# Sums of squares moved from GpSimd to VectorE at the sublayer boundaries, and the filter's last layer in the split format

## The chip, the cores and the metric

The kernel runs on one core of a Trainium2 chip. The metric is the time of one execution on the device in microseconds (us), as the median of three runs. Engines are named as the profile names them: PE is TensorE (the matrix engine; PEld its weight loads), DVE is VectorE, ACT is ScalarE, POOL is GpSimd, and SP is SyncE, whose queue issues most of the DMA transfers.

## The reference

Two layers of an encoder on 512 tokens of width 1024, in float32. Each layer has a mixer and a gated feed-forward block with a convolution, and each of these four sublayers is wrapped in a norm before and a norm after it:

```python
def rms_norm(x, gain):
    y = xf * lax.rsqrt(jnp.mean(xf * xf, axis=-1, keepdims=True) + EPS)
    return y * gain
...
for layer in range(DEPTH):
    h = rms_norm(x, mix_pre_norm[layer])
    m = even_mixer(h, ...) if layer % 2 == 0 else odd_mixer(h, ...)
    x = x + rms_norm(m, mix_post_norm[layer])
    h = rms_norm(x, ffn_pre_norm[layer])
    f = conv_ffn(h, ...)
    x = x + rms_norm(f, ffn_post_norm[layer])
```

The even mixer is latent attention beside neighbourhood attention on an 8 by 64 grid; the odd one is retention beside a Hyena operator, a long convolution done with Fourier transforms. The Hyena filters do not depend on x. They come out of a small network over the 512 positions with a window on its output:

```python
h = jnp.sin(freq * (z @ w1 + b1))
...
h = h @ w4                      # 512 x 64 times 64 x 1024
return h[:, :HY_WIDTH] * window, h[:, HY_WIDTH:] * window
```

## The kernel before, in words

**Tiles.** x and every h are eight tiles of 128 features by 512 tokens. A matrix product in the split format runs three matmuls for each 128x128 block of weights, in `mm` (L280 to L282): high part by high part, high part of the weights by low part of h, low part of the weights by high part of h. Weights arrive by DMA on SP's queue into `raw` (128x1024), and ACT makes the high part `whi` (L259) and DVE the low part `wlo` (L260). There are four buffers of weights, and three are loaded ahead.

**A boundary between two sublayers** (`boundary`, called four times; the last has no following sublayer and the change leaves it as it is). The columns are worked in two halves of 256 tokens, `ca` and `cb`. The products of the last sublayer end with half ca, its norm's statistic is taken (`stats`: matmuls with a column of ones L292, a mean on DVE L295 or L297, a power on POOL L299), the factor is spread over all partitions by PE transposes (`spread`, L316), and `update(ca)` runs for each of the eight tiles: DVE multiplies by the factor out of PSUM (L392), DVE adds x (L393), ACT writes the high part of the new h (L333) and DVE the low part (L334). Half cb follows. Meanwhile PE goes on with the next sublayer's first four tiles in halves (`proj_halves`: 192 matmuls of 256 columns, in the order ca first three k, ca the rest, cb first three k, cb the rest). The norm ahead of the next sublayer is not applied to h but later to its products, so its statistic may come late: `squares` takes the square of each new x on ACT (L404, L406) and sums them in `acc2`, by 14 adds of 128x256 on POOL (L407) at each boundary. The statistic of acc2 is taken for half ca inside the 192 matmuls and for half cb behind them, and the factor is copied to `Rb` in two halves on ACT (L442, L445).

**The three boundaries** lie at about 258 to 300 us (mixer to feed-forward, layer 0), 641 to 695 us (feed-forward of layer 0 to the mixer of layer 1; here tokens are reordered, `perm`, so that x is read with a stride) and 933 to 978 us (mixer to feed-forward, layer 1). Behind the second one the mixer loads Fourier constants `dftf` by two DMAs on POOL's queue (L934), since these cast on the way.

**The filter** (`filters`) is a generator that the feed-forward block of layer 0 steps every second output tile j. Its last layer is eight products of K=64 in plain float32 (L986), each of which the profile shows as two passes, with the window multiplied on DVE out of PSUM (L987), sum and difference of the two directions on POOL (L989), and a DMA to DRAM. PSUM tag C, which these products use, has one buffer. The rest of that block is the split product at full width.

**Order.** A list scheduler places the instructions on each engine by priorities. `high_priority` and `issue_after` shift them.

Of the kernel before, what the change touches and what calls it, by code (L numbers as in the profile page):

```python
# [10 lines left out]
F32 = mybir.dt.float32  # L11
F32R = mybir.dt.float32r
AF = mybir.ActivationFunctionType
ALU = mybir.AluOpType
AX = mybir.AxisListType

P = 128
S = 512
D = 1024
KT = D // P  # L20
# [10 lines left out]
HC = 512  # L31
# [81 lines left out]
def lay_out(inp):  # L113
# [51 lines left out]
    def ffn(l):  # L165
# [4 lines left out]
        for j in range(KT):  # L170
            for k0, k1 in ((0, 8), (8, 16), (16, 22)):
# [3 lines left out]
                pieces.append(p)  # L175

    ffn(0)
    w = inp["c_w_in"][0]
    for j in range(12):
# [7 lines left out]
    for j in range(KT):  # L187
        stat(inp["c_w_out"][0], rng(P * j, P))
    ffn(1)
    a["w"] = f32(np.stack(pieces))  # L190

# [14 lines left out]
class Body:  # L206
# [132 lines left out]
    def boundary(self, pool, tag, x, prod, gpost, gpre, ns, ftag, perm=False, rin=None):  # L339
        nc = self.nc  # L340
        new = lambda n: pool.tile([P, S], F32, tag=tag, bufs=SB[tag], name=self.nm(n))
        acc, lastsq = new("acc"), []
        fs = []
        e = None if rin is None else self.eps_over(self.small(4, "e"), rin)
        rc = lambda a: a.rearrange("p (c r) -> p r c", r=GR)
        v3 = lambda a: a.rearrange("p (r c) -> p r c", c=GW)

        def evac(k, ps, cs, full):
            n = cs.stop - cs.start
            f = fs[k][:, cs]  # L350
            if k == 0:
                nc.scalar.activation(acc[:, cs], ps, AF.Square)
            else:
                sq = new("sq")[:, :n]
                with ExitStack() if full else self.tc.high_priority(HP):
                    nc.scalar.activation(sq, ps, AF.Square)
                    if k < KT - 1 or cs.start == 0:
                        nc.vector.tensor_tensor(acc[:, cs], acc[:, cs], sq, ALU.add)
                    else:
                        lastsq.append(sq)  # L360
            nc.scalar.activation(f, ps, AF.Copy, scale=self.col(gpost + k))

        for k in range(KT - ns):
            fs.append(self.X("f", tag=ftag))
            evac(k, prod(k), slice(0, S), True)
        ca, cb = slice(0, 256), slice(256, 512)
        late = [prod(k, True) for k in range(KT - ns, KT)]
        for _ in late:
            fs.append(self.X("f", tag=ftag))
        last = gpre is None  # L370


        def own(k, cs):
            if perm:
                return rc(x[k])[:, cs.start // GW:cs.stop // GW]
            return x[k][:, cs]

        def products(cs):
            for k in range(KT - ns, KT):
                for ps in late[k - KT + ns](cs):  # L380
                    yield
                evac(k, ps, cs, False)

        def norm(cs):
            with self.tc.high_priority(HP):
                return self.stats([acc[:, cs]] + lastsq, D, 256, None if rin is None else e[:, cs.start // P:cs.stop // P])

        def update(cs, R):
            v = v3 if perm else (lambda a: a)
            for k in range(KT):  # L390
                f = fs[k][:, cs]
                nc.vector.tensor_tensor(f, f, R, ALU.mult)  # L392
                (nc.gpsimd if last and k in POOLK else nc.vector).tensor_tensor(v(f), v(f), own(k, cs), ALU.add)  # L393
                if last:
                    (nc.sync if k % 2 else nc.scalar).dma_start(self.out[k * P:(k + 1) * P, cs], f)
                    continue
                self.scaled(h[k], f, self.col(gpre + k), cs)

        def squares(cs):
            v = v3 if perm else (lambda a: a)  # L400
            for k in range(KT):
                f = fs[k][:, cs]
                if k == 0:
                    nc.scalar.activation(acc2[:, cs], f, AF.Square)  # L404
                else:
                    nc.scalar.activation(own(k, cs), v(f), AF.Square)  # L406
                    nc.gpsimd.tensor_tensor(v(acc2[:, cs]), v(acc2[:, cs]), own(k, cs), ALU.add)  # L407

        def drain(g):
            for _ in g:  # L410
                pass

        drain(products(ca))
        ra = norm(ca)
        g = products(cb)
        next(g)
        if not last:
            acc2 = new("acc2")
            h = self.new_h()
        with self.tc.issue_after(self.last_mm):  # L420
            R = self.spread(ra, "C")
        update(ca, R)
        drain(g)
        rb = norm(cb)
        if not last:
            with self.tc.issue_after(self.pow.ins):
                squares(ca)
        if last:
            update(cb, self.spread(rb, "B"))
            return fs, None, None  # L430
        g = self.proj_halves(h, ("pj", "A", "pj", "A"))
        ps = next(g)
        update(cb, self.spread(rb, "B"))
        squares(cb)
        next(g)
        self.new_factor()
        next(g)
        with self.tc.issue_after(self.last_mm):
            r = self.stats([acc2[:, ca]], D, 256, out=self.rcol[:, :2])
        drain(g)  # L440
        with self.tc.issue_after(self.last_mm):
            nc.scalar.copy(self.Rb[:, ca], self.spread(r, "C"))  # L442
            with self.tc.high_priority(HP):
                r = self.stats([acc2[:, cb]], D, 256, out=self.rcol[:, 2:])
            nc.scalar.copy(self.Rb[:, cb], self.spread(r, "C"))  # L445
        return fs, h, ps

    def gemm(self, ps, w, h, cs=slice(0, S), order=tuple(range(KT))):
# [418 lines left out]
    def ffn(self, p, x, h, pre, l):  # L867
        nc = self.nc
        a = []
        sh = GR if l == 0 else 1  # L870
        rcol, Rb = self.rcol, self.Rb
        if l == 0:

            t = self.X("Rp", tag="xa")
            nc.scalar.copy(t.rearrange("p (r c) -> p r c", c=GW), Rb.rearrange("p (c r) -> p r c", r=GR))
            ps = self.PS("B")
# [4 lines left out]

        steps = iter(())
        if l == 0:
            new = lambda n, tag, bufs: p.tile([P, S], F32, tag=tag, bufs=bufs, name=self.nm(n))
            room = [new("fa", "s", 3) for _ in range(3)] + [new("fb", "flt", 2) for _ in range(2)]
            steps = self.filters(room + [self.X("fc") for _ in range(2)])

        for j in range(FT):
            if j % 2 == 0:
# [3 lines left out]
            t, g = self.X("t"), self.X("g")  # L893
# [10 lines left out]
            if l == 0:  # L904
                cr = lambda a: a.rearrange("p (c r) -> p c r", r=GR)
                nc.vector.tensor_tensor(t.rearrange("p (r c) -> p c r", c=GW), cr(ups), cr(g), ALU.mult)
                g = t
            else:
                nc.vector.tensor_tensor(g, ups, g, ALU.mult)
            hi = p.tile([P, S], F32R, name=f"ahi{l}_{j}")  # L910
            lo = p.tile([P, S], F32R, name=f"alo{l}_{j}")
# [48 lines left out]
        nc.scalar.activation(dst, a, AF.Sin)  # L960


    def filters(self, room):
        nc = self.nc
        z, fw, w4f, w4b, fh, a, n = room
        w4 = (w4f, w4b)
        nc.sync.dma_start(z[:33], self.I["fz"])
        nc.sync.dma_start(fw[:64, :192], self.I["fw"][:64, :192])
        for d in range(2):
            nc.sync.dma_start(w4[d][:64], self.I["fw"][:64, 192 + d * HC:192 + (d + 1) * HC])  # L970
        yield
        k = 33
        for i in range(3):
            ps = self.PS("C")
            nc.tensor.matmul(ps[:64], fw[:k, 64 * i:64 * i + 64], z[:k], start=True, stop=True)
            z, fh, k = fh, z, 64
            self.sin(z[:64], ps[:64], self.cols[:64, C_FI + 1 + i:C_FI + 2 + i], self.cols[:64, C_FI:C_FI + 1], a[:64], n[:64])
            yield
        for tk in range(4):
            par, hh = tk // 2, tk % 2  # L980
            lhs = z[:64].rearrange("p (m two) -> p two m", two=2)[:, par, hh * P:hh * P + P]
            win = (a, n)
            for d in range(2):
                nc.sync.dma_start(win[d], self.I["fwin"][:, (tk * 2 + d) * HC:(tk * 2 + d + 1) * HC])
                ps = self.PS("C")
                nc.tensor.matmul(ps, lhs, w4[d][:64], start=True, stop=True)  # L986
                nc.vector.tensor_tensor(win[d], ps, win[d], ALU.mult)  # L987
            for i, (t, op) in enumerate(((fh, ALU.add), (fw, ALU.subtract))):
                nc.gpsimd.tensor_tensor(t, a, n, op)  # L989
                nc.sync.dma_start(self.filt[i, tk * P:(tk + 1) * P], t)  # L990
            yield


# [289 lines left out]
```

## Time and profile before

| | |
|---|---|
| median of three runs | 1323.95 us (1322.36 to 1324.27) |
| profiled execution | 1324.02 us, span of the trace 1321.9 us |
| PE busy | 1282.6 us, 97% of the span |
| DVE, ACT, POOL busy | 809.0, 583.1, 132.5 us |
| chain that ended last | PE 84%, DVE 7%, ACT 3%, issue 2%, DMA 2%, POOL 1% |
| mean granted clock of PE | 0.986 |

A share of busy time is a mean over stages. The stage decides: where PE has no idle time, what counts is PE's work; where it waits, the row of PE names in brackets how long it sat idle and which instruction ended that. The granted clock stands as a share of full speed, so 1.00 is 2.4 GHz and 0.50 is 1.2 GHz.

### The profile page before, as it was taken

How to read it: one execution, taken by the hardware profiler on the slowest of the kernel's cores; microseconds unless marked ns; L12 is line 12 of the kernel's file. 1: busy time of each engine (PE TensorE's matmuls, PEld its weight loads, DVE VectorE, ACT ScalarE, POOL GpSimd, SP SyncE). 2: the span in 40 equal slices, each digit the busy share in tenths (PEclk: the TensorE clock that was granted, in tenths of full speed). 3: DMA queues.
4: the chain of work that ended last, by engine and by line, in shares of the span. 5: the costliest groups of instructions: out<-in, count | busy, mean ns of one | idle time of the engine just before them, and what ended most of it. 6: DMA issues, size and time to landing. Idle time of an engine off the chain costs nothing.

```text
span 1321.9 us, 16451 instructions
## 1 busy us (share of the span) xinstructions
PE 1282.6 (97%) x6370; PEld 1062.2 (80%) x6370; DVE 809.0 (61%) x1269; ACT 583.1 (44%) x943; POOL 132.5 (10%) x126
## 2 busy tenths in 40 slices
PE   8999799999999999999889999999999999999997
PEld 7788677997877788888887878778988888888886
DVE  7679897479756555222668795775775555553223
ACT  5355798456523333222444234544553333332221
POOL 4021322040011000000230000000210000000002
PEclk9999899999999999999989999999999999999999
DMA  7222012223434322333253233213233333333331
GB/s 269 81 64 80 1 32 81 80 70 118 119 121 144 112 96 96 103 105 103 73 207 127 64 114 107 72 57 115 79 96 100 98 101 101 96 96 97 111 96 64
DMA packets 41402, 130.35 MB, mean 99 GB/s; under 512 B 4619, under 2 KB 6859, under 8 KB 40812
## 3 DMA queue, kind: packets, MB, share of 16 engines
q1 hardware_dynamic: 35708, 116.66, 27.6%
q10 hardware_dynamic: 5040, 8.45, 1.9%
q0 software_dynamic: 576, 4.19, 0.8%
q8 instruction: 50, 0.82, 0.3%
q14 instruction: 28, 0.23, 0.1%
HBM read 122.99 MB, written 6.29 MB: 98 GB/s over the span
## 4 chain that ended last, share of the span: by engine, by line
PE 84%; DVE 7%; ACT 3%; issue 2%; DMA 2%; POOL 1%; SPq 0%; DVEq 0%; ACTq 0%; POOLq 0%
PE pspj L280 16%; PE pspj L282 16%; PE pspj L281 16%; PE psA L280 9%; PE psA L282 9%; PE psA L281 9%; DVE wlo L260 2%; DVE f L393 1%; DVE h L334 1%; ACT e L792 1%; DVE f L392 1%; DMA raw<-in_w 1%; PE psB L292 1%; PE psB L669 1%; PE psB L808 1%
## 5 line engine op out<-in xcount | busy, mean ns | idle before, releaser
L259 ACT CAST whi<-raw 128x1024 fp32r<-128x1024 f32 (+1 forms) x200 | 209.2, 1048 | 437.7 <-PE pspj L281 243.0
L260 DVE TENSOR_TENSOR wlo<-raw,whi 128x1024 fp32r<-128x1024 f32 (+1 forms) x200 | 247.6, 1240 | 215.2 <-ACT whi L259 212.8
L280 PE MATMUL pspj<-h,whi 128*128 128x512 f32 (+1 forms) x664 | 251.8, 379 | 2.4 <-DVE v L597 2.3
L281 PE MATMUL pspj<-h,whi 128*128 128x512 f32 (+1 forms) x664 | 250.9, 378 | 1.4 <-DVE h L334 1.4
L282 PE MATMUL pspj<-h,wlo 128*128 128x512 f32 (+1 forms) x664 | 251.2, 378 | 0.0
L282 PE MATMUL psA<-h,wlo 128*128 128x512 f32 (+1 forms) x424 | 156.3, 369 | 4.4 <-DVE wlo L260 4.3
L280 PE MATMUL psA<-h,whi 128*128 128x512 f32 (+1 forms) x424 | 157.6, 372 | 0.0
L281 PE MATMUL psA<-h,whi 128*128 128x512 f32 (+1 forms) x424 | 155.8, 367 | 0.0
L280 PEld LDWEIGHTS pspj<-h,whi 128*128 128x128 f32 x664 | 126.5, 191 | 25.2 <-DVE v L597 2.7
L281 PEld LDWEIGHTS pspj<-h,whi 128*128 128x128 f32 x664 | 126.5, 191 | 24.0 <-DVE h L334 1.8
L282 PEld LDWEIGHTS pspj<-h,wlo 128*128 128x128 f32 x664 | 126.5, 190 | 22.5 <-issue 0.2
L280 PE MATMUL pspj<-ahi,whi 128*128 128x512 f32 x308 | 121.4, 394 | 0.0
L282 PE MATMUL pspj<-ahi,wlo 128*128 128x512 f32 x308 | 120.7, 392 | 0.0
L281 PE MATMUL pspj<-alo,whi 128*128 128x512 f32 x308 | 119.5, 388 | 0.0
L280 PEld LDWEIGHTS psA<-h,whi 128*128 128x128 f32 x424 | 81.0, 191 | 19.8 <-issue 5.4
L282 PEld LDWEIGHTS psA<-h,wlo 128*128 128x128 f32 x424 | 80.8, 191 | 19.4 <-DVE wlo L260 6.3
L281 PEld LDWEIGHTS psA<-h,whi 128*128 128x128 f32 x424 | 80.9, 191 | 12.2
L299 POOL TENSOR_TENSOR r<-v,mhalf 128x2 f32<-128x2 f32 (+1 forms) x14 | 13.7, 982 | 702.1 <-DVE v L297 543.0
L894 DVE TENSOR_TENSOR t<-psA,Rb 128x512 f32<-128x512 f32 x40 | 27.6, 690 | 87.8 <-PE psA L282 87.7
L282 PEld LDWEIGHTS pspj<-ahi,wlo 128*128 128x128 f32 x308 | 57.8, 188 | 13.6
L281 PEld LDWEIGHTS pspj<-alo,whi 128*128 128x128 f32 x308 | 57.8, 188 | 12.9
L280 PEld LDWEIGHTS pspj<-ahi,whi 128*128 128x128 f32 x308 | 57.9, 188 | 11.5
(357 smaller groups left out, 2188.4 us busy)
## 6 DMA issues: line engine op xcount, KB each, us to landing
raw<-in_w SPq DMA_DIRECT2D x198, 512.0 KB, 3.5
x<-in_xT SPq DMA_DIRECT2D x16, 256.0 KB, 4.2
fc<-in_fwin SPq DMA_DIRECT2D x8, 256.0 KB, 4.0
filt<-fa SPq DMA_DIRECT2D x8, 256.0 KB, 2.0
xspill<-f ACTq DMA_DIRECT2D x8, 256.0 KB, 2.2
sd<-filt ACTq DMA_DIRECT2D x8, 256.0 KB, 3.4
x<-xspill ACTq DMA_DIRECT2D x8, 256.0 KB, 3.0
rpb<-in_rpb SPq DMA_DIRECT2D x4, 384.0 KB, 4.8
```

What stands on the lines that cost most here:

```text
L259: nc.scalar.copy(hi[:, c], raw[:, c])
L260: nc.vector.tensor_tensor(lo[:, c], raw[:, c], hi[:, c].bitcast(F32), ALU.subtract)
L280: nc.tensor.matmul(ps, stat[0], mov[0], start=start, stop=False)
L281: nc.tensor.matmul(ps, stat[0], mov[1], start=False, stop=False)
L282: self.last_mm = nc.tensor.matmul(ps, stat[1], mov[0], start=False, stop=stop).ins
L292: nc.tensor.matmul(ps[:, j:j + 1], a[:, j * P:(j + 1) * P], self.ones, start=a is accs[0], stop=a is accs[-1])
L299: self.pow = nc.gpsimd.tensor_tensor(r, v, self.mhalf[:, :c], ALU.pow)
L334: self.nc.vector.scalar_tensor_tensor(lo, src, g, hi.bitcast(F32), ALU.mult, ALU.subtract)
L392: nc.vector.tensor_tensor(f, f, R, ALU.mult)
L393: (nc.gpsimd if last and k in POOLK else nc.vector).tensor_tensor(v(f), v(f), own(k, cs), ALU.add)
L669: tr = lambda o, i: nc.tensor.transpose(o, i, self.ident)
L894: nc.vector.tensor_tensor(t, gps, Rb, ALU.mult)
```

## The change

At the three boundaries the squares are still made on ACT, but POOL no longer adds them. Behind the second update DVE adds them as whole tiles of 128x512 (six adds L411, and one into acc2, L413). One statistic over all four column blocks stands behind the 192 matmuls in place of two over halves, and one copy writes Rb.

```diff
                 else:
                     nc.scalar.activation(own(k, cs), v(f), AF.Square)
-                    nc.gpsimd.tensor_tensor(v(acc2[:, cs]), v(acc2[:, cs]), own(k, cs), ALU.add)
+        def square_sum():
+            for k in range(2, KT):
+                nc.vector.tensor_tensor(x[1], x[1], x[k], ALU.add)
+            v = v3 if perm else (lambda a: a)
+            nc.vector.tensor_tensor(v(acc2), v(acc2), own(1, slice(0, S)), ALU.add)
...
         if not last:
-            with self.tc.issue_after(self.pow.ins):
-                squares(ca)
+            squares(ca)
...
         squares(cb)
+        square_sum()
         next(g)
         self.new_factor()
-        next(g)
-        with self.tc.issue_after(self.last_mm):
-            r = self.stats([acc2[:, ca]], D, 256, out=self.rcol[:, :2])
         drain(g)
         with self.tc.issue_after(self.last_mm):
-            nc.scalar.copy(self.Rb[:, ca], self.spread(r, "C"))
             with self.tc.high_priority(HP):
-                r = self.stats([acc2[:, cb]], D, 256, out=self.rcol[:, 2:])
-            nc.scalar.copy(self.Rb[:, cb], self.spread(r, "C"))
+                self.stats([acc2], D, out=self.rcol)
+            nc.scalar.copy(self.Rb, self.spread(self.rcol, "C"))
```

In the filter z is split into its high part on partitions 0 to 63 and its low part on 64 to 127 (`zz`), and w4 likewise into a high part, which stands in both halves, and a low part. A product is then one matmul with K=128 and one with K=64 in the split format. Sum and difference go to DVE, and the generator has one step more, so that the products come two tiles j later.

```diff
+        zz = self.X("zz", F32R)
...
+            nc.scalar.copy(hi, raw)
+            nc.vector.tensor_tensor(lo[:64], raw[:64], hi[:64].bitcast(F32), ALU.subtract)
+        yield
...
-                nc.tensor.matmul(ps, lhs, w4[d][:64], start=True, stop=True)
+                nc.tensor.matmul(ps, zz[:, ts], w4[d][0], start=True, stop=False)
+                nc.tensor.matmul(ps, zz[:64, ts], w4[d][1][:64], start=False, stop=True)
                 nc.vector.tensor_tensor(win[d], ps, win[d], ALU.mult)
-            for i, (t, op) in enumerate(((fh, ALU.add), (fw, ALU.subtract))):
-                nc.gpsimd.tensor_tensor(t, a, n, op)
-                nc.sync.dma_start(self.filt[i, tk * P:(tk + 1) * P], t)
+            nc.vector.tensor_tensor(t, a, n, ALU.add)
+            nc.vector.tensor_tensor(n, a, n, ALU.subtract)
```

Three places show how the instructions stand now. The first is DVE's queue at the end of the second boundary, from the last tile of the second update (L392, L393, L334) to the statistic's mean (L295), before:

```order
L392 TENSOR_TENSOR f_5475<-f_5475,psB_5764 128x256
L393 TENSOR_TENSOR f_5475<-f_5475,f_2567 128x256
L295 TENSOR_SCALAR v_5915<-psB_5912 128x2
L334 SCALAR_TENSOR_TENSOR h_5589<-f_5475,cols,h_5588 128x256
L260 TENSOR_TENSOR wlo_5708<-raw_5706,whi_5707 128x1024
L260 TENSOR_TENSOR wlo_5714<-raw_5712,whi_5713 128x1024
L295 TENSOR_SCALAR v_5985<-psB_5982 128x2
```

and after the change:

```order
L392 TENSOR_TENSOR f_5487<-f_5487,psB_5769 128x256
L411 TENSOR_TENSOR f_2432<-f_2432,f_2468 128x512
L393 TENSOR_TENSOR f_5487<-f_5487,f_2567 128x256
L411 TENSOR_TENSOR f_2432<-f_2432,f_2504 128x512
L411 TENSOR_TENSOR f_2432<-f_2432,f_2564 128x512
L334 SCALAR_TENSOR_TENSOR h_5601<-f_5487,cols,h_5600 128x256
L411 TENSOR_TENSOR f_2432<-f_2432,f_2565 128x512
L411 TENSOR_TENSOR f_2432<-f_2432,f_2566 128x512
L411 TENSOR_TENSOR f_2432<-f_2432,f_2567 128x512
L413 TENSOR_TENSOR acc_1047_5585<-acc_1047_5585,f_2432 128x512
L260 TENSOR_TENSOR wlo_5713<-raw_5711,whi_5712 128x1024
L260 TENSOR_TENSOR wlo_5719<-raw_5717,whi_5718 128x1024
```

The seven adds stand between the last tile of the update and the weights' low parts; three of them stand ahead of the last low part of h (L334). The second place is POOL's queue at the same boundary, where rcol is the factor of the statistic and dftfhi and dftflo are the Fourier constants; before (twelve more rows of L407 stand where lines are left out):

```order
L299 TENSOR_TENSOR r_5683<-v_5681,mhalf 128x2
L407 TENSOR_TENSOR acc_1041_5573<-acc_1041_5573,f_2432 128x256
...
L299 TENSOR_TENSOR rcol_5874<-v_5915,mhalf 128x2
L407 TENSOR_TENSOR acc_1041_5573<-acc_1041_5573,f_2567 128x256
L934 DMA dftfhi<-in_dftf 128x2048
L299 TENSOR_TENSOR rcol_5874<-v_5985,mhalf 128x2
L934 DMA dftflo<-in_dftf 128x2048
```

and after:

```order
L299 TENSOR_TENSOR r_5564<-v_5562,mhalf 128x2
L299 TENSOR_TENSOR r_5695<-v_5693,mhalf 128x2
L934 DMA dftfhi<-in_dftf 128x2048
L299 TENSOR_TENSOR rcol_5879<-v_5982,mhalf 128x4
L934 DMA dftflo<-in_dftf 128x2048
```

All adds are gone from POOL's queue, and the first DMA of constants stands ahead of the only power of the statistic. The third place is PE's queue at the first two products of the filter's last layer, before (nine more rows of psA<-h stand where lines are left out):

```order
L282 MATMUL pspj_3667<-h_2731,wlo_3563 128x512
L986 MATMUL psC_3713<-fa_3189,fb_3191 128x512
L280 MATMUL psA_3724<-h_2717,whi_3593 128x512
...
L281 MATMUL psA_3724<-h_2724,whi_3593 128x512
L282 MATMUL psA_3724<-h_2723,wlo_3594 128x512
L986 MATMUL psC_3717<-fb_3190,fb_3191 128x512
```

and after:

```order
L282 MATMUL pspj_3819<-h_2731,wlo_3714 128x512
L998 MATMUL psC_3866<-fs_3699,zz_3695 128x512
L999 MATMUL psC_3866<-w4l_3700,zz_3695 128x512
L280 MATMUL psA_3879<-h_2717,whi_3745 128x512
L281 MATMUL psA_3879<-h_2718,whi_3745 128x512
L282 MATMUL psA_3879<-h_2717,wlo_3746 128x512
L280 MATMUL psA_3879<-h_2719,whi_3745 128x512
L281 MATMUL psA_3879<-h_2720,whi_3745 128x512
L998 MATMUL psC_3871<-fs_3706,zz_3695 128x512
L999 MATMUL psC_3871<-w4l_3707,zz_3695 128x512
```

Between the two products of a pair twelve matmuls stood, and now five. Both products write the one buffer of psC, which DVE reads in between (L987 before, L1000 after).

## Rows read from the trace of the kernel before

**Rows 1.** Windows: span, busy us of PE, PEld, DVE, ACT, POOL, clock, DMA, GB/s.

```profile
360.00:445.00 85.00, 85.00 (x347) 63.58 (x346) 48.69 (x70) 26.86 (x35) 8.95 (x8) 1.00 0.38 124
...
664.00:666.00 2.00, 2.00 (x11) 2.00 (x11) 2.00 (x6) 1.01 (x2) 0.00 (x0) 0.50 0.76 248
...
950.00:952.00 2.00, 1.00 (x9) 0.80 (x8) 2.00 (x2) 0.00 (x0) 1.92 (x2) 1.00 0.00 0
```

**Rows 2.** Timeline of PE at the filter's first product: start, duration, instruction.

```profile
364.23 0.39 PE L282 MATMUL pspj<-h,wlo 128*128 128x512 f32 x1
364.54 1.13 PE L986 MATMUL psC<-fa,fb 64*128 64x512 f32 x2
...
365.94 0.40 PE L281 MATMUL psA<-h,whi 128*128 128x512 f32 x1
366.17 0.40 PE L282 MATMUL psA<-h,wlo 128*128 128x512 f32 x1
```

**Rows 3.** Timeline of DVE at the same place.

```profile
364.72 1.05 DVE L906 TENSOR_TENSOR t<-pspj,g 128x512 f32<-128x512 f32 x1 [1.71 <-PE pspj L282]
...
367.35 0.68 DVE L987 TENSOR_TENSOR fc<-psC,fc 128x512 f32<-128x512 f32 x1
```

**Rows 4.** Timeline of PE at the second boundary, idle time and its releaser in brackets.

```profile
655.08 0.38 PE L281 MATMUL pspj<-h,whi 128*128 128x256 f32 x1 [0.44 <-DVE h L334]
...
657.36 0.39 PE L281 MATMUL pspj<-h,whi 128*128 128x256 f32 x1 [0.95 <-DVE h L334]
...
660.80 0.58 PE L282 MATMUL psA<-h,wlo 128*128 128x256 f32 x1 [1.97 <-DVE wlo L260]
661.18 0.41 PE L280 MATMUL psA<-h,whi 128*128 128x256 f32 x1
...
666.94 0.32 PE L282 MATMUL psA<-h,wlo 128*128 128x256 f32 x1
...
681.07 0.28 PE L282 MATMUL psA<-h,wlo 128*128 128x256 f32 x1
681.19 0.50 PE L292 MATMUL psB<-ones,acc 128*128 128x1 f32 x4
...
692.49 0.79 PE L282 MATMUL psC<-t,dftflo 128*128 128x512 f32 x1 [2.12 <-DMA dftflo<-in_dftf]
```

**Rows 5.** Timeline of DVE at the second boundary.

```profile
650.80 0.50 DVE L334 SCALAR_TENSOR_TENSOR h<-f,cols,h 128x256 fp32r<-128x256 f32 x1
...
656.23 1.08 DVE L334 SCALAR_TENSOR_TENSOR h<-f,cols,h 128x256 fp32r<-128x256 f32 x1
657.23 0.41 DVE L392 TENSOR_TENSOR f<-f,psC 128x256 f32<-128x256 f32 x1
...
659.53 1.21 DVE L260 TENSOR_TENSOR wlo<-raw,whi 128x1024 fp32r<-128x1024 f32 x1
...
675.24 0.51 DVE L334 SCALAR_TENSOR_TENSOR h<-f,cols,h 128x256 fp32r<-128x256 f32 x1 [0.51 <-ACT h L333]
```

**Rows 6.** Timeline of POOL at the second boundary.

```profile
652.53 6.61 POOL L407 TENSOR_TENSOR acc<-acc,f 128x256 f32<-128x256 f32 x6
...
682.31 0.76 POOL L934 DMA_DIRECT2D dftfhi<-in_dftf  x1 [5.08 <-issue]
...
684.84 0.57 POOL L934 DMA_DIRECT2D dftflo<-in_dftf  x1
```

**Rows 7.** Timeline of PE at the first and the third boundary.

```profile
274.53 0.39 PE L282 MATMUL psA<-h,wlo 128*128 128x256 f32 x1 [1.01 <-DVE wlo L260]
...
951.48 0.38 PE L282 MATMUL psA<-h,wlo 128*128 128x256 f32 x1 [1.00 <-DVE wlo L260]
```

**Rows 8.** Timeline of DVE at the first boundary.

```profile
272.72 1.76 DVE L260 TENSOR_TENSOR wlo<-raw,whi 128x1024 fp32r<-128x1024 f32 x1
```

**Rows 9.** Timeline of DVE ahead of the first boundary.

```profile
246.01 0.68 DVE L358 TENSOR_TENSOR acc<-acc,sq 128x512 f32<-128x512 f32 x1
```

**Rows 10.** The instructions of line L989: durations in ns, first and last start.

```profile
L989 POOL TENSOR_TENSOR fa<-fc,fc x8: 1291/1293/1299, 370.5 to 444.9; 128x512 f32<-128x512 f32 x8
```

More of the change, by code (lines that the diff above doesn't have):

```diff
@@ L883, in ffn @@
         if l == 0:
-            new = lambda n, tag, bufs: p.tile([P, S], F32, tag=tag, bufs=bufs, name=self.nm(n))
-            room = [new("fa", "s", 3) for _ in range(3)] + [new("fb", "flt", 2) for _ in range(2)]
-            steps = self.filters(room + [self.X("fc") for _ in range(2)])
+            steps = self.filters(lambda tag, bufs, dt=F32: p.tile([P, S], dt, tag=tag, bufs=bufs, name=self.nm("f" + tag)))
         for j in range(FT):
@@ L960, in sin, with filters @@
         nc.scalar.activation(dst, a, AF.Sin)
-    def filters(self, room):
+    def filters(self, new):
         nc = self.nc
-        z, fw, w4f, w4b, fh, a, n = room
-        w4 = (w4f, w4b)
+        z, fw, fh = new("s", 3), new("s", 3), new("s", 3)
+        a, n = new("flt", 2), new("flt", 2)
         nc.sync.dma_start(z[:33], self.I["fz"])
         nc.sync.dma_start(fw[:64, :192], self.I["fw"][:64, :192])
-        for d in range(2):
-            nc.sync.dma_start(w4[d][:64], self.I["fw"][:64, 192 + d * HC:192 + (d + 1) * HC])
         yield
@@ L978, in filters @@
             yield
+        zz = self.X("zz", F32R)
+        split = lambda t: t.rearrange("p (two m) -> p two m", two=2)
+        zv = z[:64].rearrange("p (m two) -> p two m", two=2)
+        nc.scalar.copy(split(zz[:64]), zv)
+        nc.vector.tensor_tensor(split(zz[64:]), zv, split(zz[:64].bitcast(F32)), ALU.subtract)
+        w4 = []
+        for d in range(2):
+            raw, hi, lo = self.X("w4"), new("s", 3, F32R), self.X("w4l", F32R)
+            for half in (raw[:64], raw[64:]):
+                nc.sync.dma_start(half, self.I["fw"][:64, 192 + d * HC:192 + (d + 1) * HC])
+            nc.scalar.copy(hi, raw)
+            nc.vector.tensor_tensor(lo[:64], raw[:64], hi[:64].bitcast(F32), ALU.subtract)
+            w4.append((hi, lo))
+        yield
         for tk in range(4):
-            par, hh = tk // 2, tk % 2
-            lhs = z[:64].rearrange("p (m two) -> p two m", two=2)[:, par, hh * P:hh * P + P]
-            win = (a, n)
+            ts = slice(tk * P, tk * P + P)
+            win, t = (a, n), new("s", 3)
             for d in range(2):
@@ L985, in filters @@
                 ps = self.PS("C")
-                nc.tensor.matmul(ps, lhs, w4[d][:64], start=True, stop=True)
+                nc.tensor.matmul(ps, zz[:, ts], w4[d][0], start=True, stop=False)
+                nc.tensor.matmul(ps, zz[:64, ts], w4[d][1][:64], start=False, stop=True)
                 nc.vector.tensor_tensor(win[d], ps, win[d], ALU.mult)
-            for i, (t, op) in enumerate(((fh, ALU.add), (fw, ALU.subtract))):
-                nc.gpsimd.tensor_tensor(t, a, n, op)
-                nc.sync.dma_start(self.filt[i, tk * P:(tk + 1) * P], t)
+            nc.vector.tensor_tensor(t, a, n, ALU.add)
+            nc.vector.tensor_tensor(n, a, n, ALU.subtract)
+            for i, src in enumerate((t, n)):
+                nc.sync.dma_start(self.filt[i, ts], src)
             yield
```

## The prediction

> **What bounds the kernel now.** I read the page first: PE is busy for 97% of the span, and the chain that ended last is PE for 84% of it. So time can come from two sources only: work taken off PE where PE has no idle time, and idle or slowly clocked time of PE. I then cut the trace into windows by stage to see which holds where the change acts.
>
> The filter's products lie inside 360 to 445 us. There PE is busy for 85.00 of 85.00 us at a clock of 1.00 [rows 1], so what the filter saves on PE is saved in full, and what other engines do there costs nothing until PE waits for it. DVE has 36 us to spare in that window, ACT 58.
>
> The three boundaries I read on the timelines of PE, DVE and POOL. At the second one PE waits three times in the first half of the next projection, for 0.44, 0.95 and 1.97 us, and each time DVE is named: twice a low part of h, once a low part of a weight [rows 4]. Behind the third wait the matmuls of 256 columns start every 0.213 us ((666.94 - 661.18) / 27, 28 matmuls from the first to the last) [rows 4], where the last ones before the statistic stand 0.12 us apart (681.07 to 681.19) [rows 4]; the granted clock there is 0.50, the level of 1.2 GHz [rows 1]. At the first and the third boundary PE waits once, for 1.01 and 1.00 us, for a low part of a weight [rows 7], and the clock stays at 1.00 around the latter [rows 1].
>
> Why is DVE late? POOL's row gives it: from 652.53 us on, six of its adds stand back to back for 6.61 us [rows 6]. DVE's L334 takes 0.50 us just before and 1.08 within that stretch, while L392, which reads one operand from PSUM, takes 0.41 there [rows 5]. At the first boundary the low part of a weight takes 1.76 us [rows 8] beside 1.21 elsewhere [rows 5]. So instructions of DVE that take all operands from SBUF take twice as long, or 0.55 us more, while POOL adds, and PE waits for just these.
>
> **The change, part by part.** All sums go against the profiled execution's 1324.02 us, which is 0.07 us above the median of the three runs.
>
> *Filter, minus 5.0 us.* From L282 at 364.23 to the second matmul behind L986 at 365.94 are 1.71 us; two steps at the usual pitch of 0.23 (365.94 to 366.17) [rows 2] would be 0.46. So one plain product costs PE 1.25 us, and eight cost 10.0. In their place come 16 matmuls of 512 columns in the split format. The trace has none with K=64 or with K=128 of this kind; as the nearest I take the pitch of the other split matmuls, 0.23, together 3.7 us, and as a dear bound 0.31, the step from 364.23 to 364.54, where the kind of matmul changes [rows 2]: 5.0 us. Then there is a new wait. The second product of a pair stands only five matmuls behind the first, and psC has one buffer, so it waits for DVE's window product (L1000) of the first. With the first at 364.54, PE comes to the second at about 364.54 + 7 x 0.23 = 366.1. DVE's L906 runs from 364.72 to 365.77, and a window product takes 0.68 [rows 3], so psC is free at about 366.4: a wait of 0.35, four times, 1.4 us. Bounds: nothing, and 0.9 each where DVE is at something else. Sum: -10.0 + 3.7 + 1.4 = -4.9, which I carry as -5.0; between -1.4 (5.0 and 3.6) and -6.3. The split of z and w4, the sums and differences (eight more instructions of some 0.68 us [rows 9]) and the loads of w4, which go later in SP's queue, lie beside busy PE; POOL's eight of 1.29 us [rows 10] go, and no one on PE waited for them.
>
> *Second boundary, minus 5.8 us.* With POOL's queue empty DVE's instructions take their short times. About one instruction of DVE is lengthened for each add that it meets; five of them stand between 652.53 and the weight's low part at 659.53, at 0.58 each (1.08 - 0.50) [rows 5] 2.9 us, an estimate. That low part then ends at 660.74 - 2.9 = 657.8 instead of 660.74. PE, without its first two waits, comes there at 660.80 - 1.97 - 0.95 - 0.44 = 657.4. A wait of 0.4 is left of 3.36: -2.9. Each of the three restarts also carries a first matmul of 0.38 rather than 0.28 [rows 4], 0.1 each; I count two: -0.2. Then the clock: 27 steps at 0.213 rather than 0.12, 2.5 us, and 0.2 for the first; if PE does not sit idle for so long, the clock does not fall: -2.7. Together -5.8. Bounds: -6.3 (no wait left), and -3.1 (the clock falls nevertheless). Behind it the two waits for the Fourier constants stay: their DMAs start at 682.31 and 684.84 [rows 6], just behind the statistic at 681.19, and PE waits 2.12 us for the second [rows 4]. The first is released by the statistic's last read of acc2, in both kernels, so it moves with PE.
>
> *First and third boundary, minus 1.1 each.* The one wait of 1.0 us [rows 7] ends with a weight's low part that is itself 0.55 too long [rows 8], and two or three instructions ahead of it are lengthened alike (0.5 each); so it comes more than 1.0 us earlier, and the wait goes, with 0.1 of restart. Bounds: 0 and -1.2.
>
> *The seven adds on DVE, nothing.* An add of 128x512 from SBUF takes 0.68 us [rows 9], so seven take 4.8, of which three stand ahead of the update's last instruction. At the second boundary the update ends at 675.75 [rows 5] now; with the 2.9 us of the first half and six lengthened instructions in the second (3.5 us, an estimate as above) it ends at about 669.4, and the adds end at 674.2 at the latest. PE ends its 192 matmuls at 681.2 - 5.8 = 675.4. So the cover is about 1.2 us or more. Without the cover every late microsecond is paid: the statistic, the factor Rb and both DMAs of constants stand behind the adds. The two low parts of weights that stand behind the adds wait for buffers that the 192 matmuls free, not for DVE.
>
> *One statistic, plus 0.3.* The four column blocks are multiplied by ones once in either kernel; moving two of them behind the drain shifts at most the 0.50 us of such a row [rows 4] from before the end of the 192 matmuls to after it: no change. One copy of 512 columns delivers Rb later than the second of two copies of 256 did. A row of each width on DVE, 0.41 [rows 5] and 0.68 [rows 9], says 0.27; I take it once, since PE has nine matmuls of the next tile as cover. Bounds: 0 and 0.9.
>
> Sum: -5.0 - 5.8 - 1.1 - 1.1 + 0.3 = -12.7, so 1324.0 - 12.7 = **1311.3 us**. All dear bounds together give -1.4 - 3.1 + 0.9 = -3.6 (1320.4); all cheap ones -6.3 - 6.3 - 1.2 - 1.2 = -15.0 (1309.0).
>
> **The clock, weighed.** The rows say: three waits of together 3.36 us within 6 us, then the level of 1.2 GHz; one wait of 1.0 us, and the level stays. The remaining 0.4 us is below both. The Trainium skill ("TensorE: Matmul & The Clock Gate", section "What's actually happening") says that the slow level is the default, which activity lifts, and that the number of slow matmuls differs from run to run. By that rule a short wait can be paid dearly in one run and not in another; the sum would be 1314.0 without the clock's 2.7. The trace agrees in so far as a wait of 1.0 us left the clock alone, so I keep the gain and give the other case a chance of its own.
>
> **The rivals.**
>
> *The clock falls at the second boundary all the same* (0.20). For it: PE still waits there for DVE, which runs two low parts of weights between the updates. Against it: rows 1 and 7. Then 1311.3 + 2.7 = **1314.0 us**.
>
> *The filter's gain is eaten by waits for psC* (0.10). For it: one buffer, and only five matmuls between the products of a pair. Against it: DVE has 36 us of slack, and L906 ends early. At the dear bound of 1.4 instead of 5.0: **1314.9 us**.
>
> *The adds land on the path; slower* (0.06). If DVE's long instructions come from their own operands (strides, ACT's writes to the same tiles) and not from POOL, none of them gets shorter, and the update ends at 675.75 as now. An add would then be priced by the row of the same shape that met another engine, 1.29 us [rows 10]: seven take 9.0, end at 684.8, and come 3.6 us behind the end of the 192 matmuls at 681.2. The room is about the same at the other boundaries, an estimate: thrice 3.6 is 10.8. With the filter's -5.0 that is +5.8: **1329.8 us**. It decides from the point where the adds end later than the last of the 192 matmuls; up to there they cost nothing. Against it: L392 with an operand from PSUM is not lengthened in the same stretch, and L334 of the same shape is short just before POOL starts [rows 5, 6]. The Trainium skill ("SBUF — State Buffer", section "SBUF: two separate sides") speaks against this rival too: DVE with two operands from SBUF and GpSimd reading SBUF exclude each other for a whole instruction. By that rule an add costs 0.68 once POOL is empty, and the rival is worth nothing. The rows of DVE agree.
>
> *Nothing happens* (0.04). The boundaries only exchange waits (a later factor and a statistic of four blocks against the waits at the weights), and the filter gives its dear bound: 1324.0 - 1.4 = **1322.6 us**, within 0.2%.
>
> **How the numbers follow.** The forecast has 0.60, the three cases above on the faster side (with the one of the clock and the one of psC) 0.90 together, no change 0.04, slower 0.06. A difference of 0.2%, or 2.6 us, is about what a measurement of this kernel can tell from no change. The range reaches from 1306, some 3 us below the cheap bounds since DVE's relief may also shorten waits that I don't count, to 1318, which takes in both faster rivals and one further miss of 3 us; it leaves out the last two.
>
> **What the changed profile would show.** At the second boundary: no POOL adds, L334 at 0.5 us throughout, one wait of PE of under 1 us, the clock at 1.00 from 655 us to the statistic, and L413 ended a microsecond before the ones-matmuls. At the other two: no wait of 1 us for wlo. In the filter: 16 matmuls 0.23 us apart, with four waits of some 0.35 us for psC, and the span from 360 us to the end of that block shorter by 5 us. It is wrong if PE waits for L413, if the clock falls between the updates, or if a wait for psC is nearer 1 us.

## The result and the profile after

The changed kernel takes 1308.20 us (median of six runs, 1306.86 to 1312.44) against 1322.49 (six runs) before, 14.3 us less: a ratio of 0.9895, 95% interval 0.9878 to 0.9912. The forecast was 1311.3, 12.7 us less, with a range of 1306 to 1318. Every ratio below is likewise against the kernel before as it was timed beside that run (medians of 1321.45 to 1322.29 us). The profiled execution took 1307.53 us with a span of 1305.8, 16.1 less than the span before.

The timeline of PE at the second boundary after the change, to be held against [rows 4]:

```profile
651.66 0.38 PE L282 MATMUL psA<-h,wlo 128*128 128x256 f32 x1 [0.75 <-DVE wlo L260]
...
668.92 0.94 PE L292 MATMUL psB<-ones,acc 128*128 128x1 f32 x8
...
676.93 0.47 PE L280 MATMUL psC<-t,dftfhi 128*128 128x512 f32 x1 [0.53 <-DMA dftfhi<-in_dftf]
...
680.10 0.50 PE L282 MATMUL psC<-t,dftflo 128*128 128x512 f32 x1 [2.24 <-DMA dftflo<-in_dftf]
```

Of three waits of together 3.36 us one of 0.75 is left, and the first matmul behind it takes 0.38 us, not 0.58. DVE in the same place, against [rows 5]:

```profile
649.42 0.49 DVE L334 SCALAR_TENSOR_TENSOR h<-f,cols,h 128x256 fp32r<-128x256 f32 x1
...
650.37 1.24 DVE L260 TENSOR_TENSOR wlo<-raw,whi 128x1024 fp32r<-128x1024 f32 x1
...
664.66 2.21 DVE L411 TENSOR_TENSOR f<-f,f 128x512 f32<-128x512 f32 x3
666.91 1.13 DVE L413 TENSOR_TENSOR acc<-acc,f 128x512 f32<-128x512 f32 x1
```

L334 keeps its short time. The last add, strided here, ends at 668.04, 0.9 us ahead of the ones-matmuls at 668.92 that read its result; this lead is called the cover. At the first boundary the cover is 4.2 us:

```profile
284.93 0.69 DVE L413 TENSOR_TENSOR acc<-acc,x 128x512 f32<-128x512 f32 x1
```

```profile
289.80 0.95 PE L292 MATMUL psB<-ones,acc 128*128 128x1 f32 x8
```

There the wait of 1.01 us [rows 7] is gone; the third boundary is alike. The windows (columns as in [rows 1]) show the clock at 1.00 behind the wait:

```profile
650.00:652.00 2.00, 1.25 (x10) 1.05 (x9) 2.00 (x4) 0.93 (x2) 0.00 (x0) 1.00 0.00 0
652.00:654.00 2.00, 2.00 (x19) 2.00 (x18) 2.00 (x7) 0.66 (x2) 0.00 (x0) 1.00 0.53 141
```

The filter's first pair of products on PE, against [rows 2]:

```profile
383.39 0.39 PE L282 MATMUL pspj<-h,wlo 128*128 128x512 f32 x1
383.61 0.40 PE L998 MATMUL psC<-fs,zz 128*128 128x512 f32 x1
383.94 0.50 PE L999 MATMUL psC<-w4l,zz 64*128 64x512 f32 x1
384.37 0.50 PE L280 MATMUL psA<-h,whi 128*128 128x512 f32 x1
384.71 0.40 PE L281 MATMUL psA<-h,whi 128*128 128x512 f32 x1
384.94 0.39 PE L282 MATMUL psA<-h,wlo 128*128 128x512 f32 x1
...
385.64 0.41 PE L998 MATMUL psC<-fs,zz 128*128 128x512 f32 x1
```

The steps around the 64-row matmul L999 are not 0.23 but 0.33, 0.43 and 0.34, and the second L998 follows 0.24 us behind its predecessor: no wait for psC.

Where the 16 us came from is read by pairing PE's rows of both traces in their order and taking the difference of their starts (worked out; negative is earlier after the change):

| up to here in the trace before | shift | this stage |
|---|---|---|
| 199 us, first mixer, which the change doesn't touch | -1.48 | -1.48 |
| behind the wait at the first boundary | -2.61 | -1.13 |
| end of the feed-forward block with the filter | -5.99 | -3.38 |
| behind the third wait at the second boundary (660.80) | -9.14 | -3.15 |
| clock back at 1.00 there (670) | -11.84 | -2.70 |
| behind the statistic (685) | -11.74 | +0.10 |
| second wait for the constants (692.49) | -12.39 | -0.65 |
| 701 us, behind a stretch at 1.2 GHz that is missing now | -14.86 | -2.47 |
| ahead of the third boundary (+1.4 and -1.5 of clock between) | -14.90 | -0.04 |
| behind the third boundary, and to the end | -16.05 | -1.15 |

The stages with a term in the forecast give -11.4 (-1.13 - 3.38 - 3.15 - 2.70 + 0.10 - 1.15). The other -4.6 are a shorter wait for the constants and stretches of clock that one execution has and the next has not; the six runs of the changed kernel spread over 5.6 us.

### The profile page after: what moved, and what is told of

Read it like the earlier page. It is cut to its first block, busy times and chain, and to the rows that moved or that the text cites. A ratio compares the mean times of both kernels' runs of the same rounds, so it can differ in the third digit from the quotient of the medians.

```text
span 1305.8 us, 16380 instructions
## 1 busy us (share of the span) xinstructions
PE 1271.7 (97%) x6370; PEld 1057.5 (81%) x6370; DVE 813.9 (62%) x1298; ACT 582.9 (45%) x943; POOL 80.9 (6%) x73
## 4 chain that ended last, share of the span: by engine, by line
PE 87%; DVE 5%; ACT 3%; issue 2%; DMA 1%; POOL 1%; SPq 0%; DVEq 0%; POOLq 0%; ACTq 0%
PE pspj L280 17%; PE pspj L282 17%; PE pspj L281 17%; PE psA L280 10%; PE psA L282 10%; PE psA L281 10%; DVE wlo L260 1%; ACT e L794 1%; DMA raw<-in_w 1%; PE psB L292 1%; PE psB L671 1%; PE psB L810 1%; DVE h L334 1%; ACT whi L259 1%; PE psC L282 1%
## 5 line engine op out<-in xcount | busy, mean ns | idle before, releaser
L260 DVE TENSOR_TENSOR wlo<-raw,whi 128x1024 fp32r<-128x1024 f32 (+1 forms) x200 | 246.6, 1235 | 204.8 <-ACT whi L259 202.8
```

Of the source, the lines that this page charges most:

```text
L260: nc.vector.tensor_tensor(lo[:, c], raw[:, c], hi[:, c].bitcast(F32), ALU.subtract)
```

## The experiments

The theory: GpSimd's adds double the time of DVE's instructions beside them, and PE waits for these; taken away, PE runs on, as long as DVE's adds end ahead of the statistic. Rivals: the new order or the single statistic makes the gain; and for the filter, other costs than PE's columns.

**One part alone.** The first kernel has the changed boundaries with the old filter, the second the new filter with the old boundaries; no other edit.

> The changed boundaries with the old filter. Theory: the boundaries' gain does not depend on the filter. The three waits at the second boundary (0.44, 0.95, 1.97 us) shrink to one of about 0.75, the clock does not fall there, the single waits of 1.0 us at the first and third go: 8 to 11 us under the kernel before, 1312 to 1314. Rival: the filter's change is needed for it (its loads and its adds on GpSimd lie ahead in the same queues); then one of the waits at the second boundary stays and the time is above 1316.

> The new filter with the old boundaries. Theory: PE saves 3.5 us in the filter's block, as the trace of the changed kernel shows, and all waits of the boundaries stand as before: 1319. Rival: the 5.0 us forecast come out where the boundaries are the old ones: 1317.5. If the filter moved the boundaries, one of the waits 0.44, 0.95 and 1.97 would be gone.

The boundaries alone: 1314.01 us (ratio 0.994, 0.9918 to 0.9961). At the second boundary one wait of 0.74 us is left, the clock stays up, and the waits of 1.0 us at the others are gone; the rival that the filter is needed for this is out.

```profile
655.16 0.39 PE L282 MATMUL psA<-h,wlo 128*128 128x256 f32 x1 [0.74 <-DVE wlo L260]
```

The filter alone: 1317.39 (0.9971, 0.9955 to 0.9987), with the waits of before:

```profile
649.47 0.38 PE L281 MATMUL pspj<-h,whi 128*128 128x256 f32 x1 [0.45 <-DVE h L334]
...
651.78 0.39 PE L281 MATMUL pspj<-h,whi 128*128 128x256 f32 x1 [0.97 <-DVE h L334]
...
655.16 0.58 PE L282 MATMUL psA<-h,wlo 128*128 128x256 f32 x1 [1.93 <-DVE wlo L260]
```

By paired rows its block saves 3.4 us, not 5.0; the time still lies below the theory's 1319, since the start of the profiled execution alone is 2.3 us shorter, mostly by clock. The two parts add up: by paired rows the boundaries alone give -1.2, -5.7 and -1.2 us and the filter alone -3.4, together the -11.4 of the whole change.

**The adds on GpSimd again, all else as changed.**

```diff
                     nc.scalar.activation(own(k, cs), v(f), AF.Square)
+                    nc.gpsimd.tensor_tensor(v(acc2[:, cs]), v(acc2[:, cs]), own(k, cs), ALU.add)
...
-            squares(ca)
+            with self.tc.issue_after(self.pow.ins):
+                squares(ca)
...
-        square_sum()
```

> The changed kernel, but the 14 half-width adds of each boundary stand on GpSimd again, as before; the single statistic, the single copy of Rb and the new filter stay. Theory: the adds on GpSimd alone make the waits. The three waits at the second boundary (0.44, 0.95, 1.97 us), the fall of the clock behind them and the waits of 1.0 us at the first and the third come back: 1317 to 1319, the time of the kernel with the new filter alone. Rival: the single statistic or the new order of the squares gives part of the gain; then a wait is missing and the time is 1310 to 1315.

This edit also puts back the point from which the squares of half ca are released (`issue_after`); the next kernel leaves that as changed. The time is 1315.88 us (0.9965, 0.9947 to 0.9983), between the theory's 1317 and the rival's 1315. The waits are back at all three boundaries (1.00 and 1.01 at the first and third), and so most of the loss; the single statistic gave none of it. But the clock did not fall this time, which the theory had. PE's timeline and a window behind it:

```profile
650.80 0.38 PE L281 MATMUL pspj<-h,whi 128*128 128x256 f32 x1 [0.45 <-DVE h L334]
...
653.10 0.38 PE L281 MATMUL pspj<-h,whi 128*128 128x256 f32 x1 [0.97 <-DVE h L334]
...
656.49 0.38 PE L282 MATMUL psA<-h,wlo 128*128 128x256 f32 x1 [1.93 <-DVE wlo L260]
```

```profile
656.00:658.00 2.00, 1.51 (x12) 1.51 (x13) 2.00 (x4) 0.27 (x2) 1.03 (x1) 1.00 0.38 39
```

The same three waits as in the kernel with the new filter alone, to 0.01 us, where the same window stands at 0.50:

```profile
656.00:658.00 2.00, 2.00 (x11) 2.00 (x11) 2.00 (x7) 0.58 (x2) 0.00 (x0) 0.50 0.87 236
```

So the waits are set by the adds, and the waits alone do not settle whether the clock falls. They do bear on it, as far as these profiles go: two of the three with these three waits in full have the fall, and none of the ten with a single wait of about 0.75 us there has it between that wait and the statistic.

**Adds and memsets whose result nobody reads,** beside the changed boundary: 12 adds with two reads of SBUF at each, or 14 memsets.

```diff
+                    if k > 1:
+                        nc.gpsimd.tensor_tensor(v(self.junk), own(k, cs), own(k, cs), ALU.add)
```

```diff
+            with self.tc.issue_after(self.pow.ins):
+                for _ in range(NMS):
+                    nc.gpsimd.memset(self.junk, 0.0)
```

> The changed kernel with 12 adds of 128x256 on GpSimd at each boundary, each released by a square as before, whose result nobody reads (two reads from SBUF, a small write). Theory: GpSimd's reads of SBUF lengthen DVE's instructions, whatever the result is for: L334 at about 1.0 us instead of 0.5 in their time, PE's waits at all three boundaries and the fall of the clock come back: 1316 to 1319. Rival: the waits came from somebody who waited for acc2; then nothing changes, 1308 to 1310.

> The changed kernel with 14 memsets of 128x256 on GpSimd at each boundary, starting where the adds started. They write SBUF and read nothing. Theory: reading is what lengthens DVE's instructions, so they keep their short times and PE waits as in the changed kernel: 1308 to 1311. Rival: any instruction of GpSimd on SBUF does it; then L334 takes about 1.0 us beside the memsets and waits of PE come back.

The adds: 1315.28 us (0.9961, 0.9944 to 0.9979). L334 (one line lower here, L335) is long again on DVE:

```profile
650.24 0.93 DVE L335 SCALAR_TENSOR_TENSOR h<-f,cols,h 128x256 fp32r<-128x256 f32 x1
651.09 1.13 DVE L394 TENSOR_TENSOR f<-f,f 128x256 f32<-128x256 f32 x1
```

PE waits again, twice for the low part of h and once for that of a weight:

```profile
651.22 0.38 PE L282 MATMUL pspj<-h,whi 128*128 128x256 f32 x1 [0.38 <-DVE h L335]
...
653.09 0.39 PE L282 MATMUL pspj<-h,whi 128*128 128x256 f32 x1 [0.54 <-DVE h L335]
...
655.78 0.39 PE L283 MATMUL psA<-h,wlo 128*128 128x256 f32 x1 [1.23 <-DVE wlo L261]
```

It waits another 1.77 us for DVE's last add, which comes late in turn. This is less than expected: at the first and third boundary only 0.21 us of wait is back, not 1.0, the clock stays up, and by paired rows the three boundaries lose 4.6 us against the changed kernel, where the real adds lost 8.3. The memsets: 1308.95 us (0.9927, 0.9901 to 0.9953). POOL and DVE:

```profile
648.15 5.10 POOL L436 MEMSET junk<- 128x256 bf16 x14
```

```profile
649.35 0.50 DVE L335 SCALAR_TENSOR_TENSOR h<-f,cols,h 128x256 fp32r<-128x256 f32 x1
```

Fourteen writes on POOL over 5.1 us lengthen nothing, and by paired rows no boundary loses anything against the changed kernel. It is adds that read SBUF on GpSimd that do it, not writes, and no one waited for acc2; an instruction on GpSimd that reads SBUF without being an add was not run. The Trainium skill ("SBUF — State Buffer", section "SBUF: two separate sides") names this pair: DVE with two inputs in SBUF against a GpSimd operation that reads SBUF; the runs agree in both halves.

**How far the adds are covered.** Four more adds of 128x512 in DVE's chain at each boundary; and DVE's seven whole-tile adds (L411, L413) moved to GpSimd.

```diff
+            for op in (ALU.add, ALU.subtract) * 2:
+                nc.vector.tensor_tensor(x[1], x[1], x[7], op)
```

```diff
-                nc.vector.tensor_tensor(x[1], x[1], x[k], ALU.add)
+                nc.gpsimd.tensor_tensor(x[1], x[1], x[k], ALU.add)
...
-            nc.vector.tensor_tensor(v(acc2), v(acc2), own(1, slice(0, S)), ALU.add)
+            nc.gpsimd.tensor_tensor(v(acc2), v(acc2), own(1, slice(0, S)), ALU.add)
```

> The changed kernel with four more adds of 128x512 on DVE in the chain to acc2 at each boundary (they add and subtract the same tile). In the changed kernel the last add ends 4.2, 0.9 and 4.2 us ahead of the statistic's first matmul. Theory: adds cost nothing up to that cover and everything beyond. Four times 0.74 is 3.0: no wait at the first and the third boundary, a wait of about 2.0 us at the second: 1310 to 1311, and up to 3 more if the clock falls. Rival: each add costs its time wherever it stands (DVE is what sets the pace): 3.0 us at each boundary, 1317.

> The changed kernel, but the seven whole-tile adds of each boundary stand on GpSimd behind the second update, not on DVE. Theory: an add takes 1.29 us there against 0.7; started where DVE's started, seven end 4 us later. At the first and the third boundary that is within the cover of 4.2 us, at the second it is 3 us or more beyond it; the waits of the first half stay away, since GpSimd is empty then. The statistic at the second boundary is late by 3 us or more, and the constants' DMAs behind it too: 1312 to 1318. Rival: leaving the first half free is all that matters: 1308 to 1310.

Four more adds: 1316.31 us (0.996, 0.9942 to 0.9978), nothing at the first and third boundary, and at the second:

```profile
672.04 1.02 PE L292 MATMUL psB<-ones,acc 128*128 128x1 f32 x8 [1.96 <-DVE acc L415]
...
683.80 0.77 PE L280 MATMUL psC<-t,dftfhi 128*128 128x512 f32 x1 [4.63 <-DMA dftfhi<-in_dftf]
```

The 1.96 us are about what the cover of 0.9 leaves of 3.0. The time misses the forecast of 1310 to 1311 and lies near the rival's 1317, but the rival, 3.0 us at each boundary, is out: the first and the third lose nothing. What I had not expected is the second row: the high constants land 10.0 us after their issue here and 6.3 in the changed kernel, so a statistic that is 2 us late cost 6 us, and a stretch at 1.2 GHz besides. The DMA engines were no slower: from issue to landing they moved 346 GB/s here and 319 there. But POOL's queue, which carries the constants of 1 MB each, moved 2.03 MB in that time and not 1.06, and SP's weights 1.42 and not 0.96, so most of the low constants came in before the last of the high ones. Why they were mixed so here is not shown.

On GpSimd: 1315.83 us (0.9951, 0.9935 to 0.9967). The first halves stay free (one wait of 0.79 at the second boundary), the first and third boundary lose nothing, and at the second PE waits for POOL:

```profile
672.70 1.05 PE L292 MATMUL psB<-ones,acc 128*128 128x1 f32 x8 [1.64 <-POOL acc L413]
```

So adds that end behind the 192 matmuls do land on the path, as the prediction's slower rival had it, at half the 3 us expected here, since POOL's adds start earlier, between the updates (at 660.44 us, where DVE's would start at about 663.7 in this trace). By paired rows another 1.9 us of this profile's loss stand at its start, 1.4 just behind the statistic and 2.3 behind the first wait for the constants, all clock.

**The filter's steps.** Both matmuls at K=128 (the low part of w4 in both halves, so the product of the two low parts is added); then also PSUM tag B, with two buffers, in place of C.

```diff
-            nc.vector.tensor_tensor(lo[:64], raw[:64], hi[:64].bitcast(F32), ALU.subtract)
+            nc.vector.tensor_tensor(lo, raw, hi.bitcast(F32), ALU.subtract)
...
-                nc.tensor.matmul(ps, zz[:64, ts], w4[d][1][:64], start=False, stop=True)
+                nc.tensor.matmul(ps, zz[:, ts], w4[d][1], start=False, stop=True)
```

```diff
-                ps = self.PS("C")
+                ps = self.PS("B")
```

> The changed kernel, but the second matmul of each filter product runs with K=128 too (the low part of w4 in both halves; it adds the product of the two low parts). Theory: a matmul of 64 rows between matmuls of 128 rows costs 0.41 us in slower steps on either side (0.33, 0.43 and 0.34 instead of 0.23), whatever it computes; with 128 rows all steps are 0.23, eight products save 3.3 us: about 1305 and the steps seen in the trace. Rival: the steps come from the change of PSUM tile or of the operands; then they stay and the time is that of the changed kernel, 1308.

> The changed kernel with both matmuls of a filter product at K=128 and the products in the PSUM tag B, which has two buffers and is free in this block, so that the two products of a pair stand together and wait for nothing. Theory: 16 steps of 0.23 us are all that is left; against the kernel before the block saves 8 x 1.25 - 3.6 = 6.4 us, against the changed one 2.9, where K=128 alone saved 1.65: about 1305. Rival: the wait for DVE only moves to the first product of the next pair or to the weights; then a wait stays in the block and it saves under 2 us.

With K=128 alone the block saves 1.5 us more by paired rows (the 1.65 just above is a little too much), less than half of what I expected; the time is 1309.57 us, not 1305, within the spread of the changed kernel, since this profile lost 3.3 us of clock elsewhere:

```profile
385.20 0.40 PE L998 MATMUL psC<-fs,zz 128*128 128x512 f32 x1
385.44 0.40 PE L999 MATMUL psC<-w4l,zz 128*128 128x512 f32 x1
385.68 0.39 PE L280 MATMUL psA<-h,whi 128*128 128x512 f32 x1
...
386.60 0.40 PE L281 MATMUL psA<-h,whi 128*128 128x512 f32 x1
387.15 0.51 PE L998 MATMUL psC<-fs,zz 128*128 128x512 f32 x1 [0.15 <-DVE fflt L1000]
```

The slow steps are gone, so 64 rows cost them; the wait for psC is there now (a step of 0.55 us to the second L998, where the changed kernel has 0.24; 0.15 of it is idle), since PE arrives earlier. With two buffers it goes too:

```profile
383.63 0.40 PE L998 MATMUL psB<-fs,zz 128*128 128x512 f32 x1
383.87 0.40 PE L999 MATMUL psB<-w4l,zz 128*128 128x512 f32 x1
384.11 0.39 PE L998 MATMUL psB<-fs,zz 128*128 128x512 f32 x1
384.34 0.39 PE L999 MATMUL psB<-w4l,zz 128*128 128x512 f32 x1
384.57 0.40 PE L280 MATMUL psA<-h,whi 128*128 128x512 f32 x1
```

The block saves 3.2 us against the changed kernel, and the time is 1304.82 us (1303.70 to 1305.37; 0.987 of before, 0.9844 to 0.9896). Its four runs lie below all six of the changed kernel, which were timed apart from them, and the intervals of the two ratios just overlap; but the profiled executions differ by 3.3 us, and nearly all of that is in this block. So it is the fastest of these kernels.

**The waits for the constants.** The DMA of the low constants goes first; then also the factor's spread in PSUM tag B; then that with the filter of 1304.82.

```diff
+        for i in (1, 0):
+            with self.tc.high_priority(1000):
+                self.nc.gpsimd.dma_start(out[i].rearrange("p m a b -> p (m a b)"), self.I[name][:, i * 2048:(i + 1) * 2048])
```

```diff
-            nc.scalar.copy(self.Rb, self.spread(self.rcol, "C"))
+            nc.scalar.copy(self.Rb, self.spread(self.rcol, "B"))
```

> The changed kernel, but the DMA of the low Fourier constants goes ahead of that of the high ones. It waits for nothing that the boundary does and was held by the queue alone. Theory: PE's wait of 2.24 us for it ends and the wait of 0.53 for the high part does not grow: 2 to 3 us less, 1305 to 1306. Rival: the early transfer meets the weights' transfers and a wait for a weight takes its place, or the high part lands no earlier and PE waits the same sum for it: 1307 to 1309.

> The low Fourier constants first, as in the earlier run, and the spread of the norm's factor in PSUM tag B instead of C, so that the first spectrum product does not wait for the copy of Rb on ACT. Theory: in the earlier run the wait of 3.21 us was for that copy, which stood behind a weight's cast; without it only a wait of about 0.5 us for the high constants is left of 2.8, and the clock stays up: 2 to 4 us under the changed kernel, 1304 to 1306. Rival: the high constants land no earlier than before and PE waits some 3 us for them: 1308 to 1310.

> Both of the above in one kernel. Theory: the gains add, since one lies in the feed-forward block and the other behind the second boundary: 2.9 and 2.2 to 4 us under the changed kernel, 1301 to 1303. Rival: the second wait only moves: 1305.

1310.27, 1310.40 and 1308.46 us: no gain, three misses, and the last is 3.6 us slower than its filter alone made it. The first kernel has lost the wait of 2.24 us and found one of 3.21:

```profile
681.33 0.50 PE L280 MATMUL psC<-t,dftfhi 128*128 128x512 f32 x1 [3.21 <-ACT Rb L447]
```

The scheduler had put the copy of Rb behind one more weight's cast on ACT, which waited 2.83 us for its DMA. With the spread in another bank PE passes there with a wait of 1.12 us for the high constants, and stops at the next tile, at 684.74, for 2.15 us. The profile names the small DVE instruction behind L1076; L1076, which multiplies that PSUM buffer by Rb, runs from 683.91 to 684.59, behind the low part of a weight (L260, from 682.77) and the copy of Rb (from 682.64). Both stand behind the cast of that weight on ACT, which had waited 2.85 us for its DMA. So the wait only moved, and what sets it is now a weight's transfer. The spread in tag B also added a wait of 0.23 us at the first boundary, with a fall of the clock behind it, together 3.7 us in that profile.

## Why the prediction was right, point by point

**Contention, right.** DVE's instructions with two operands in SBUF are long beside GpSimd's adds and short without them, shown by taking the adds away, putting them back, and putting back adds without a reader. The last of these brought back long instructions (0.93 us at the second boundary), but the waits only in part.

**First and third boundary, right:** -1.13 and -1.15 for -1.1 each.

**Second boundary, right in sum, one part with luck.** The waits gave -3.15 for a forecast of -3.1 (2.9 and 0.2), with 0.75 us left where I had worked out 0.4. The clock gave -2.70 as forecast, but the profile of before need not have had that fall: the same waits without it are in the run with the adds on GpSimd again. I gave the clock 0.20 as a rival on the side of the changed kernel, where no profile has the fall; the doubt belonged to the kernel before.

**Adds, right and narrow.** The cover was 0.9 us at the second boundary for a forecast of 1.2. The strided last add took 1.13 us, which no row of before had shown, and adds in a chain start every 0.74 us, where I had 0.68.

**Filter, the mechanism right and the size off.** -3.38 for -5.0. The mis-sized term is "16 matmuls at 0.23, together 3.7": a product of L998 and L999 cost 0.46 + 0.41, eight 6.9 us, beyond the dear bound of 5.0. The waits for psC (1.4) did not occur, because the slow steps gave DVE the time, and so half of the miss was paid back. The run with K=128 shows both halves: without the slow steps the wait returns, and the sum comes to the 4.9 us that were worked out (3.4 + 1.5).

**One statistic:** 0.1 for 0.3. At the first and third boundary PE now waits 0.41 and 0.40 us for POOL's power; the shift behind it is the same as ahead of the statistic, so what left the 192 matmuls pays for it. The forecast had neither; the two about cancel.

**Constants:** I had said that both waits stay. They shrank by 0.65 us, and the stretch at 1.2 GHz behind them was missing in this profile, 2.47 us more. With the 1.48 us of the start this is 4.6 us that no term of the forecast holds. The terms fell short by 1.3 (11.4 for 12.7), which took part of it away, and so 1311.3 lies 3.8 us above the profiled 1307.53. By the terms alone the time would be 1312.6, in the range too; that it came so near the forecast is in part two misses going opposite ways. The stretches are no effect of the change that I can show: a kernel with the same boundaries (the run of them alone) has the one behind the constants. I had also said that the statistic's last read of acc2 releases the first DMA. The changed profile names a cast on ACT (L274) for it; the runs with a late statistic name the ones-matmuls.

## What to carry to other kernels

An accumulation on GpSimd that reads SBUF is not free when PE waits for DVE beside it: look at the mean of DVE's instructions inside and outside GpSimd's stretches. Moved to DVE it is free only up to the next reader, so take the end of the last add against that reader at each place, and count what is queued behind the reader, DMAs above all. Here a matmul among others of 128 rows was cheaper with all 128 rows, though half of its work was spare.

## What the runs showed of the hardware

A matmul of 64 rows between matmuls of 128 rows took three slow steps (0.33, 0.43 and 0.34 us), about 0.4 us more than three of 0.23; with 128 rows it took its 0.23. Memsets on GpSimd left DVE's L334 at 0.50 us; the adds into acc2 made it 1.08, those without a reader 0.93. The granted clock did not follow from PE's idle time alone: it stayed at 1.00 through waits of 0.45, 0.97 and 1.93 us in one run and fell to 0.50 within the third of the same waits in another, and in the run with the spread in tag B it fell behind 0.42 and 0.23 us and eight matmuls of one column, where the changed kernel, without the 0.23, stayed at 1.00.
